# Seven-product tiles whose first product moves from one PSUM bank to another

## The chip, the cores and the metric

The kernel runs on one core of one Trainium2 chip. The metric is the time of one execution on the device in microseconds (us). TensorE (PE in the profile, with PEld for its weight loads) multiplies, VectorE (DVE) and ScalarE (ACT) do the elementwise work, GpSimd (POOL) and SyncE (SP) mostly issue DMAs.

## The reference

One inference step of a two-layer decoder on 512 prompt tokens and 8 sample tokens, width 1024, hidden width 2816. Each layer has two SwiGLU blocks around a token mixer, so there are four such blocks:

```python
def _swiglu(x, wg, wu, wd):
    return (jax.nn.silu(x @ wg) * (x @ wu)) @ wd
...
        x = x + 0.5 * _swiglu(_rmsnorm(x, norm_g[l, 0]), ffn_w_gate[l, 0], ffn_w_up[l, 0], ffn_w_down[l, 0])
        h = _rmsnorm(x, norm_g[l, 1])
        if l < N_A_LAYERS:
            out, nbuf = _pool_mixer(h, pool_bufs[l], pos0, pool_w[l], pool_scale[l])
...
            out = _window_attention(q, kk, vv, wb, pos0, attn_sinks[j]) @ w_o[j]
        x = x + out
        x = x + 0.5 * _swiglu(_rmsnorm(x, norm_g[l, 2]), ffn_w_gate[l, 1], ffn_w_up[l, 1], ffn_w_down[l, 1])
```

The change touches the four SwiGLU blocks alone; the pooling mixer, the attention and the norms stay as they are.

## The kernel before

Everything is held transposed: a tile has 128 features on the partitions and 520 tokens (512 + 8) in the free dimension; a half tile has 260 tokens (H). To keep float32 precision each operand is split into a high and a low part in the matmul's format, and a product of two blocks is three matmuls per 128 rows of the contraction: high by high, low by high, high by low. The weights are split as they arrive: ACT writes the high part (wh, line 287), DVE the low part (wl, line 288).

The hidden width of 2816 is 22 tiles, in three parts of 8, 8 and 6 (PARTS). The first 4, 3, 2 and 2 tiles of the four blocks are computed plainly (plain_tile). The others go through strassen_tile: it takes the gate and the up column block of a tile together as a 2 x 2 block matrix and multiplies it by the two token halves with seven block products instead of eight. The down projection of the parts of 8 tiles goes through strassen_down in the same manner, two output tiles at a time. One call of product is 12 matmuls of 128x260. In the order of the code the seven products are called, after their moving operand, B11, T1, T2, B21, B22, T3 and T4.

PSUM has eight banks, used as four pairs (duo). A tile takes two pairs: one bank of the first pair is a, in which B11, T2, T3 and T4 are accumulated one after the other; the second pair is c. B11 goes to a and ACT copies it to the first half of sa in SBUF (line 794, in strassen_down 831). T1 goes to the second bank of c and ACT copies it to sb (799, 833). T2 is accumulated onto a and ACT copies the sum to the second half of sa (802, 839). B21 goes to the first bank of c as a fresh sum, B22 is accumulated onto T1 in the second bank. Then DVE adds sa to both banks of c, 520 columns (806, 846), multiplies by the norm's factor R (809, 847), and ACT takes the silu (810); in strassen_down DVE adds the result to the residual instead (848). T3 is accumulated onto a, and DVE adds a to sb (812, 850). T4 is accumulated onto a after that, by a closure (rest) that runs when the next tile is under way; it ends in two DVE multiplications (815, 817; 855, 857), after which DVE and ACT make the operands of the down projection (hidden). The products onto a follow each other through its evacuations: T2 waits for the first copy, T3 for the second, T4 for the DVE addition to sb.

strassen_tile with early=True, the first such tile of each of the four blocks, goes another way, with one bank more.

Nothing in these blocks has an order written by hand. A scheduler takes the program, keeps its data dependences and its buffers, and lays the instructions of each engine out in an order of its own before the run; each engine then works through its list in order. So matmuls of several products are often woven into each other. Only the attention (PLAN) and some norms keep the written order.

Of the kernel before, what the change touches and what calls it, by code (L numbers as in the profile page):

```python
# [11 lines left out]
F32 = mybir.dt.float32  # L12
# [3 lines left out]
ALU = mybir.AluOpType  # L16
AX = mybir.AxisListType

P = 128
# [5 lines left out]
TOK = SP + NS  # L25
TW = TOK + NS
H = TOK // 2
# [297 lines left out]
def yoco_step(ctx, tc, ins, outs):  # L325
# [4 lines left out]
    V, S, T = nc.vector, nc.scalar, nc.tensor  # L330
# [19 lines left out]
    def duo():  # L350

        cnt[0] += 1
        return pools[0].tile([P, 2, 512], F32, tag="ps", name=f"ps{cnt[0]}")
# [178 lines left out]
    R = cp.tile([P, TOK], F32, name="R")  # L532

    def hcols(t, hf):
        return t[:, hf * H : (hf + 1) * H]


    def halves(t):
        return t.rearrange("p (h b a) -> p h b a", h=2, b=2)

    def two(z):

        return z.rearrange("p (b a) -> p a b", b=2)

    def back(z):

        return z.rearrange("p (b a) -> p b a", b=2)

    def outs(banks):

        return banks[:, :, :H].rearrange("p h (a b) -> p h b a", b=2)

    def out(bank):

        return bank[:, :H].rearrange("p (a b) -> p b a", b=2)
# [52 lines left out]
    def terms(w, xx):  # L608
        return ((w[0], xx[0]), (w[0], xx[1]), (w[1], xx[0]))
# [31 lines left out]
    def product(mov, bank, more=False):  # L641


        w = W.get()
        W.prefetch()
        for kk in range(4):
            for i, (a, b) in enumerate(terms(w, mov[kk])):
                T.matmul(  # L648
                    bank[:, :H],
                    a[:, kk, :],  # L650
                    two(b),
                    start=(not more and kk == 0 and i == 0),
                    stop=(kk == 3 and i == 2),
                    skip_group_check=more,
                )

    def hidden(g, hs):
        hs.take(g)
# [118 lines left out]
    def finish():  # L777
        if unfinished:
            unfinished.pop()()

    def strassen_tile(tmp, xx, tt, hs, early=False):

        B = lambda src, ks, hf: [tuple(hcols(z, hf) for z in src[k]) for k in ks]
        lo, up = range(4), range(4, 8)
        g = tmp.tile([P, TOK], F32, tag="g", name="g")
        t = tmp.tile([P, TOK], F32, tag="t", name="t")
        sa = tmp.tile([P, TOK], F32, tag="sa", name="sa")
        sb = tmp.tile([P, H], F32, tag="sb", name="sb", bufs=2)  # L790
        both, c = duo(), duo()
        a, b = both[:, 0, :], both[:, 1, :] if early else c[:, 1, :]
        product(B(xx, lo, 0), a)
        S.copy(back(hcols(sa, 0)), out(a))
        if early:
            product(B(xx, up, 0), c[:, 0, :])
            product(B(xx, up, 1), c[:, 1, :])
        product(B(tt, lo, 0), b)
        S.copy(back(sb), out(b))  # L799
        finish()  # L800
        product(B(tt, lo, 1), a, True)
        S.copy(back(hcols(sa, 1)), out(a))
        if not early:
            product(B(xx, up, 0), c[:, 0, :])
            product(B(xx, up, 1), c[:, 1, :], True)
        V.tensor_tensor(halves(g), halves(sa), outs(c), op=ALU.add)
        if early:
            V.tensor_tensor(hcols(g, 1), hcols(g, 1), sb, op=ALU.add)
        V.tensor_tensor(g, g, R, op=ALU.mult)
        S.activation(t, g, AF.Silu)  # L810
        product(B(tt, up, 0), a, True)
        V.tensor_tensor(back(sb), back(sb), out(a), op=ALU.add)

        def rest():
            V.tensor_tensor(hcols(g, 1), sb, hcols(t, 1), op=ALU.mult)
            product(B(tt, up, 1), a, True)
            V.tensor_tensor(back(hcols(g, 0)), out(a), back(hcols(t, 0)), op=ALU.mult)
            hidden(g, hs)

        unfinished.append(rest)  # L820

    def strassen_down(tmp, hs):

        b, st = hs.b, {}

        def head(i):
            a, c = duo()[:, 0, :], duo()
            sa = tmp.tile([P, TOK], F32, tag="sa", name="sa")
            sb = tmp.tile([P, H], F32, tag="sb", name="sb", bufs=2)
            product(b["B11"], a)  # L830
            S.copy(back(hcols(sa, 0)), out(a))
            product(b["T1"], c[:, 1, :])
            S.copy(back(sb), out(c[:, 1, :]))
            st[i] = a, c, sa, sb

        def second(i):
            a, c, sa, sb = st[i]
            product(b["T2"], a, True)
            S.copy(back(hcols(sa, 1)), out(a))

        def third(i):
            a, c, sa, sb = st[i]
            product(b["B21"], c[:, 0, :])
            product(b["B22"], c[:, 1, :], True)
            u = tmp.tile([P, TOK], F32, tag="u", name="u", bufs=nu[0])
            V.tensor_tensor(halves(u), halves(sa), outs(c), op=ALU.add)
            V.tensor_tensor(u, u, R, op=ALU.mult)
            V.scalar_tensor_tensor(x[2 * i], u, -0.5, x[2 * i], op0=ALU.mult, op1=ALU.add)
            product(b["T3"], a, True)
            V.tensor_tensor(back(sb), back(sb), out(a), op=ALU.add)  # L850

        def rest(i):
            a, c, sa, sb = st.pop(i)
            u = tmp.tile([P, TOK], F32, tag="u", name="u", bufs=nu[0])
            V.tensor_tensor(hcols(u, 1), sb, hcols(R, 1), op=ALU.mult)
            product(b["T4"], a, True)
            V.tensor_tensor(back(hcols(u, 0)), out(a), back(hcols(R, 0)), op=ALU.mult)
            V.scalar_tensor_tensor(x[2 * i + 1], u, 0.5, x[2 * i + 1], op0=ALU.mult, op1=ALU.add)

        head(0)  # L860
        finish()
        head(1)
        second(0)
        third(0)
        second(1)
        rest(0)
        third(1)
        for i in range(2, KT // 2):
            head(i)
            rest(i - 1)  # L870
            second(i)
            third(i)
        unfinished.append(lambda: rest(KT // 2 - 1))
# [24 lines left out]
    def ffn(fi, tmp, mov, hooks, tt, tags, after, before_last=None, first=None, by_parts=None, hold=False):  # L898

        j = 0  # L900
        for pi, n in enumerate(PARTS):
# [3 lines left out]
            for _ in range(n):  # L905
                if j == 0 and first is not None:
                    plain_end(tmp, *first, hs)
                elif j < NPL[fi]:
                    plain_tile(tmp, mov, hs, hooks)
                else:  # L910
                    while hooks:
                        hooks.pop(0)()
                    strassen_tile(tmp, mov, tt, hs, j == NPL[fi])
                j += 1
                W.pin = lambda ins: ins
# [1198 lines left out]
```

## Time and profile before

| | |
|---|---|
| Median of 3 runs | 1533.73 us (1533.15 to 1533.79) |
| The profiled execution's own time | 1532.24 us |
| Its span, first to last instruction | 1530.5 us |
| PE busy | 1507.7 us (99%), 13338 matmuls |
| DVE busy | 1406.7 us (92%), 2791 instructions |
| ACT busy | 969.2 us (63%), 2030 instructions |
| POOL busy | 309.6 us (20%) |
| TensorE clock granted | 0.999 of full speed |
| DMA | 255.43 MB, mean 167 GB/s |

An engine's busy time is the time in which at least one of its instructions runs. A matmul of 128x260 is shown with a duration of about 0.28 us, but the next starts about 0.11 us after it, so PE also counts as busy in short gaps between starts: the starts say more than the busy share. Likewise a DVE instruction on 520 columns is shown with about 0.70 us, and the next may start 0.60 us after it. A row "A <- B" of the waits says that A's engine was idle and that B ended the idleness.

### The profile page before, as it was taken

To read this page: it belongs to the slowest core of one execution; us is meant where nothing else is said; L and a number is where in the kernel's file an instruction comes from. 1 tells how busy PE (TensorE), PEld (TensorE's weight loads), DVE (VectorE), ACT (ScalarE), POOL (GpSimd) and SP (SyncE) were. 2 spreads that over 40 slices of the span, in tenths; PEclk is the share of its full clock that TensorE was granted. 3 is DMA by queue.
4 is the path that set the end of the run, shared out by engine and by line. 5 is a ranking of instruction groups with operands and counts; after the bars stand their busy time and mean duration, and the time that the engine had idled before them with its cause. 6 is when DMAs were issued, how large, how long until landed. Compare 5 with 4: busy or idle time off the path is not lost. (4 is left out here: it accounts for less than half of the span.)

```text
span 1530.5 us, 35121 instructions
## 1 busy us (share of the span) xinstructions
PE 1507.7 (99%) x13338; PEld 1492.0 (97%) x13338; DVE 1406.7 (92%) x2791; ACT 969.2 (63%) x2030; POOL 309.6 (20%) x348
## 2 busy tenths in 40 slices
PE   9999999999999999999999999999999999999997
PEld 9999999999999999999999999999999999999997
DVE  6999999979999999989899999987897999999976
ACT  6765665657665665656665665655886765665555
POOL 1122222101121222100321222201561122222200
PEclk9999999999999999999999999999999999999999
DMA  9689989754688989845889998953334588998941
GB/s 248 123 190 200 190 190 200 182 170 119 139 196 182 196 193 196 176 129 129 206 188 193 189 199 188 183 173 88 86 72 103 126 178 188 196 192 191 197 133 57
DMA packets 420037, 255.43 MB, mean 167 GB/s; under 512 B 13182, under 2 KB 400246, under 8 KB 419828
## 3 DMA queue, kind: packets, MB, share of 16 engines
q1 hardware_dynamic: 339918, 187.56, 44.5%
q0 software_dynamic: 76192, 60.53, 28.2%
q10 hardware_dynamic: 3758, 5.09, 1.1%
q8 instruction: 105, 1.72, 0.5%
q14 instruction: 64, 0.52, 0.1%
HBM read 218.59 MB, written 6.11 MB: 147 GB/s over the span
## 5 line engine op out<-in xcount | busy, mean ns | idle before, releaser
L287 ACT ACTIVATE wh<-raw 128x512 fp32r<-128x512 f32 (+1 forms) x770 | 445.7, 616 | 242.2 <-DVE raw L221 80.0
L288 DVE TENSOR_TENSOR wl<-raw,wh 128x512 fp32r<-128x512 f32 (+1 forms) x770 | 503.0, 679 | 37.9 <-ACT wh L287 34.3
L648 PE MATMUL ps<-th,wh 128*128 128x260 f32 x1232 | 338.5, 276 | 0.6 <-ACT sb L799 0.4
L648 PE MATMUL ps<-th,wl 128*128 128x260 f32 x1232 | 337.2, 275 | 0.5 <-DVE wl L288 0.5
L648 PE MATMUL ps<-tl,wh 128*128 128x260 f32 x1232 | 337.6, 275 | 0.0
L648 PE MATMUL ps<-xh,wh 128*128 128x260 f32 x908 | 248.8, 276 | 1.2 <-ACT wh L287 0.9
L648 PE MATMUL ps<-xh,wl 128*128 128x260 f32 x908 | 248.3, 275 | 0.5 <-DVE wl L288 0.4
L648 PE MATMUL ps<-xl,wh 128*128 128x260 f32 x908 | 248.2, 275 | 0.0
L648 PEld LDWEIGHTS ps<-th,wh 128*128 128x128 f32 x1232 | 234.0, 190 | 2.0 <-ACT wh L287 0.9
L648 PEld LDWEIGHTS ps<-tl,wh 128*128 128x128 f32 x1232 | 234.1, 190 | 0.0
L648 PEld LDWEIGHTS ps<-th,wl 128*128 128x128 f32 x1232 | 233.3, 190 | 0.7 <-DVE wl L288 0.7
L398 POOL DMA_DIRECT2D S<-in_ffn_w_up_dram x77 | 102.2, 1327 | 429.3 <-DMA S<-in_ffn_w_up_dram 130.8
L648 PE MATMUL ps<-hh,wh 128*128 128x260 f32 x656 | 180.1, 278 | 3.5 <-ACT wh L287 1.7
L648 PE MATMUL ps<-hl,wh 128*128 128x260 f32 x656 | 179.2, 276 | 0.9 <-DVE hl L380 0.9
L648 PE MATMUL ps<-hh,wl 128*128 128x260 f32 x656 | 178.3, 275 | 0.0
L214 POOL DMA_DIRECT2D raw<-raw x109 | 96.1, 882 | 399.1 <-DVE wl L288 122.2
L648 PEld LDWEIGHTS ps<-xh,wh 128*128 128x128 f32 x908 | 172.2, 190 | 2.2 <-ACT wh L287 1.5
L648 PEld LDWEIGHTS ps<-xh,wl 128*128 128x128 f32 x908 | 171.9, 190 | 1.0 <-DVE wl L288 1.0
L648 PEld LDWEIGHTS ps<-xl,wh 128*128 128x128 f32 x908 | 172.2, 190 | 0.1
L648 PEld LDWEIGHTS ps<-hh,wh 128*128 128x128 f32 x656 | 124.0, 190 | 5.5 <-ACT wh L287 2.3
L648 PEld LDWEIGHTS ps<-hl,wh 128*128 128x128 f32 x656 | 124.2, 190 | 1.6 <-DVE hl L380 1.6
L648 PEld LDWEIGHTS ps<-hh,wl 128*128 128x128 f32 x656 | 123.9, 190 | 0.0
(369 smaller groups left out, 3608.1 us busy)
## 6 DMA issues: line engine op xcount, KB each, us to landing
raw<-in_ffn_w_gate_dram SPq DMA_DIRECT2D x87, 512.0 KB, 4.5
raw<-in_ffn_w_up_dram SPq DMA_DIRECT2D x87, 512.0 KB, 6.4
raw<-in_ffn_w_down_dram SPq DMA_DIRECT2D x128, 256.0 KB, 5.0
raw<-raw POOLq DMA_DIRECT2D x109, 256.0 KB, 4.2
S<-in_ffn_w_up_dram SPq DMA_DIRECT2D x77, 256.0 KB, 4.7
S<-in_ffn_w_up_dram POOLq DMA_DIRECT2D x77, 256.0 KB, 5.6
raw<-in_ffn_w_down_dram SPq DMA_DIRECT2D x16, 768.0 KB, 4.3
S<-in_ffn_w_down_dram SPq DMA_DIRECT2D x32, 256.0 KB, 3.1
```

The lines of the kernel that those rows point to most:

```text
L214: G.dma_start(blk(raw, 2, 1), blk(raw, 1, 1), accum_op=ALU.add)
L287: pin(nc.scalar.activation(dh, src, AF.Copy))
L288: pin(nc.vector.tensor_tensor(dl, src, dh.bitcast(F32), op=ALU.subtract))
L398: return [ld(lambda t: t, a), lambda t: nc.gpsimd.dma_start(t, b, accum_op=ALU.add)]
L648: T.matmul(bank[:, :H], a[:, kk, :], two(b), start=(not more and kk == 0 and i == 0), stop=(kk == 3 and i == 2), skip_group_check=more,)
```

## The change

In the seven-product tiles other than the early ones, the first copy of ACT no longer goes to SBUF but to the first bank of c, and B21 is accumulated onto it instead of starting a fresh sum. The second copy, of B11 + T2, goes to SBUF as before. DVE then adds it to the second bank of c only, in place, 260 columns instead of 520, and the multiplication by R reads both banks of c from PSUM (520 columns) instead of a tile in SBUF. The copies keep the order of the columns as it lies in the bank instead of changing it; the multiplication changes it. Of 77 calls of strassen_tile four are early and stay as they are, so 73 tiles change there and 32 in strassen_down, 105 in all.

```diff
         product(B(xx, lo, 0), a)
-        S.copy(back(hcols(sa, 0)), out(a))
         if early:
+            S.copy(back(hcols(sa, 0)), out(a))
             product(B(xx, up, 0), c[:, 0, :])
             product(B(xx, up, 1), c[:, 1, :])
+        else:
+            S.copy(c[:, 0, :H], a[:, :H])
         product(B(tt, lo, 0), b)
         S.copy(back(sb), out(b))
         finish()
         product(B(tt, lo, 1), a, True)
...
+        else:
+            S.copy(hcols(sa, 1), a[:, :H])
+            product(B(xx, up, 0), c[:, 0, :], True)
             product(B(xx, up, 1), c[:, 1, :], True)
+            V.tensor_tensor(c[:, 1, :H], hcols(sa, 1), c[:, 1, :H], op=ALU.add)
+            V.tensor_tensor(halves(g), outs(c), halves(R), op=ALU.mult)
...
             product(b["B11"], a)
-            S.copy(back(hcols(sa, 0)), out(a))
+            S.copy(c[:, 0, :H], a[:, :H])
             product(b["T1"], c[:, 1, :])
...
-            product(b["B21"], c[:, 0, :])
+            product(b["B21"], c[:, 0, :], True)
             product(b["B22"], c[:, 1, :], True)
             u = tmp.tile([P, TOK], F32, tag="u", name="u", bufs=nu[0])
-            V.tensor_tensor(halves(u), halves(sa), outs(c), op=ALU.add)
-            V.tensor_tensor(u, u, R, op=ALU.mult)
+            V.tensor_tensor(c[:, 1, :H], sa, c[:, 1, :H], op=ALU.add)
+            V.tensor_tensor(halves(u), outs(c), halves(R), op=ALU.mult)
```

The number of instructions is the same on every engine. The order on SP is the same, POOL's differs in a few rows; PE's, DVE's and ACT's were laid out anew by the scheduler, since c is now written first by ACT and the DVE additions are shorter.

What changes in the waits: c is one tile of two banks for the program's tracking of dependences, and its first writer is now the copy. In all 105 tiles the first matmul of T1, which writes the other bank of c, waits for the count that the copy's end raises. Before, no matmul into c waited for a copy. Here is PE's list at the end of B11 and the start of T1, in a tile of the second block whose a is ps_7822 and whose c is ps_7823. Before:

```order
L648 MATMUL ps_7822<-xh,wh 128x260
L648 MATMUL ps_7822<-xl,wh 128x260
L648 MATMUL ps_7822<-xh,wl 128x260
L648 MATMUL ps_7823<-th,wh 128x260 [waits DVE_49]
L648 MATMUL ps_7823<-tl,wh 128x260
L648 MATMUL ps_7823<-th,wl 128x260
```

T1 follows B11 without a wait for ACT. In the changed kernel:

```order
L648 MATMUL ps_7822<-xh,wh 128x260
L648 MATMUL ps_7822<-xl,wh 128x260
L648 MATMUL ps_7822<-xh,wl 128x260
L648 MATMUL ps_7823<-th,wh 128x260 [waits DVE_49,Activation_49]
L648 MATMUL ps_7823<-tl,wh 128x260
L648 MATMUL ps_7823<-th,wl 128x260
```

The rows are the same, and the first of T1 now waits for ACT's copy of what the row above it completes. Of the 105 tiles, 19 have no matmul of another product between the end of B11 and the start of T1, one has 1, one has 3, 12 have 7, one has 10, and the others 12 or more. (Before, 44 tiles had none there either, and in 44 others T1 was begun ahead of B11's end.)

The second place is PE's list at the end of B22 in the last output tiles of a strassen_down in the second block (a is ps_8974, c is ps_8975; ps_9115 and ps_9116 are a and c of the next tile). Before:

```order
L648 MATMUL ps_8975<-hh,wl 128x260
L648 MATMUL ps_9115<-xh,wh 128x260 [waits PE_49,Activation_49]
L648 MATMUL ps_9115<-xl,wh 128x260
L648 MATMUL ps_9116<-th,wh 128x260 [waits PE_49,Activation_49]
L648 MATMUL ps_9116<-tl,wh 128x260
L648 MATMUL ps_9115<-xh,wl 128x260 [waits DVE_49]
```

In the changed kernel:

```order
L648 MATMUL ps_8975<-hh,wl 128x260
L648 MATMUL ps_9115<-xh,wl 128x260 [waits DVE_49]
L648 MATMUL ps_9115<-xh,wh 128x260
L648 MATMUL ps_8974<-ph,wh 128x260 [waits Activation_49]
L648 MATMUL ps_8974<-pl,wh 128x260
L648 MATMUL ps_8974<-ph,wl 128x260
```

Before, B11, T1 and T2 of the next tile were woven in here, so that 48 matmuls stood between the end of B22 and the start of T4. In the changed kernel T3 follows at once, then eight matmuls of the next tile, and T4 stands 22 matmuls after the end of B22. That is so in 12 tiles of strassen_down and in 25 of strassen_tile. Before, four tiles had 22 or fewer and the other 101 had 32 or more.

T4 waits for DVE's addition of a to sb, and this is DVE's list at the same place, before:

```order
L846 TENSOR_TENSOR u<-sa,ps_8975 128x520 [waits PE_49,Activation_49]
L847 TENSOR_TENSOR u<-u,R 128x520 [waits DVE_49]
L288 TENSOR_TENSOR wl<-raw_8801,wh 128x512 [waits Activation_49]
L850 TENSOR_TENSOR sb<-sb,ps_8974 128x260 [waits PE_49]
L848 SCALAR_TENSOR_TENSOR x_87<-u,x_87 128x520 [waits DVE_49]
```

and in the changed kernel:

```order
L851 TENSOR_TENSOR ps_8975<-sa,ps_8975 128x260 [waits PE_49]
L852 TENSOR_TENSOR u<-ps_8975,R 128x520 [waits DVE_49]
L288 TENSOR_TENSOR wl<-raw_8801,wh 128x512 [waits Activation_49]
L853 SCALAR_TENSOR_TENSOR x_87<-u,x_87 128x520 [waits DVE_49]
L855 TENSOR_TENSOR sb<-sb,ps_8974 128x260 [waits PE_49]
```

The addition to sb, on which T4 waits, moved behind the addition to the residual. In the 25 tiles of strassen_tile the list from the addition to c (813) to the addition to sb (817) is L813, L814, a split L288 and L817, with the split in the second or the third place.

More of the change, by code (lines that the diff above doesn't have):

```diff
@@ L801, in strassen_tile @@
         product(B(tt, lo, 1), a, True)
-        S.copy(back(hcols(sa, 1)), out(a))
-        if not early:
-            product(B(xx, up, 0), c[:, 0, :])
+        if early:
+            S.copy(back(hcols(sa, 1)), out(a))
+            V.tensor_tensor(halves(g), halves(sa), outs(c), op=ALU.add)
+            V.tensor_tensor(hcols(g, 1), hcols(g, 1), sb, op=ALU.add)
+            V.tensor_tensor(g, g, R, op=ALU.mult)
+        else:
+            S.copy(hcols(sa, 1), a[:, :H])
+            product(B(xx, up, 0), c[:, 0, :], True)
             product(B(xx, up, 1), c[:, 1, :], True)
[L806 to L809, printed above, removed]
+            V.tensor_tensor(c[:, 1, :H], hcols(sa, 1), c[:, 1, :H], op=ALU.add)
+            V.tensor_tensor(halves(g), outs(c), halves(R), op=ALU.mult)
         S.activation(t, g, AF.Silu)
@@ L827, in head @@
             a, c = duo()[:, 0, :], duo()
-            sa = tmp.tile([P, TOK], F32, tag="sa", name="sa")
+            sa = tmp.tile([P, TOK], F32, tag="sa", name="sa")[:, :H]
             sb = tmp.tile([P, H], F32, tag="sb", name="sb", bufs=2)
             product(b["B11"], a)
-            S.copy(back(hcols(sa, 0)), out(a))
+            S.copy(c[:, 0, :H], a[:, :H])
             product(b["T1"], c[:, 1, :])
@@ L838, in second @@
             product(b["T2"], a, True)
-            S.copy(back(hcols(sa, 1)), out(a))
+            S.copy(sa, a[:, :H])
         def third(i):
             a, c, sa, sb = st[i]
-            product(b["B21"], c[:, 0, :])
+            product(b["B21"], c[:, 0, :], True)
             product(b["B22"], c[:, 1, :], True)
             u = tmp.tile([P, TOK], F32, tag="u", name="u", bufs=nu[0])
-            V.tensor_tensor(halves(u), halves(sa), outs(c), op=ALU.add)
-            V.tensor_tensor(u, u, R, op=ALU.mult)
+            V.tensor_tensor(c[:, 1, :H], sa, c[:, 1, :H], op=ALU.add)
+            V.tensor_tensor(halves(u), outs(c), halves(R), op=ALU.mult)
             V.scalar_tensor_tensor(x[2 * i], u, -0.5, x[2 * i], op0=ALU.mult, op1=ALU.add)
```

## The prediction

> **What bounds the kernel now.** I read the page's first part, then the waits of PE, then the busy times by stretch, then the groups of the instructions that change, then two short pieces of the timeline.
>
> ```profile
> span 1530.5 us, 35121 instructions
> PE 1507.7 (99%) x13338; PEld 1492.0 (97%) x13338; DVE 1406.7 (92%) x2791; ACT 969.2 (63%) x2030; POOL 309.6 (20%) x348
> ```
>
> PE is full, so only what makes PE wait can change the time, and nothing that is taken off DVE or ACT pays by itself. These are PE's longest waits at the seven-product line 648, and ACT's for PE at the first copy:
>
> ```profile
> PE ps L648 <- ACT wh L287: 2.6, 3, 0.9
> PE ps L648 <- DVE wl L288: 1.0, 2, 0.5
> PE ps L648 <- DVE hl L380: 0.9, 2, 0.5
> PE ps L648 <- DVE g L817: 0.8, 3, 0.3
> PE ps L648 <- ACT sa L839: 0.7, 3, 0.2
> ...
> ACT sa L794 <- PE ps L648: 57.7, 42, 2.1
> ```
>
> They are few and short. Where they lie shows in the busy times by stretch (PE, PEld, DVE, ACT and POOL, us and number of instructions, then the clock, the DMA share and GB/s). Two quiet stretches first, then the eight stretches where one part of a block goes over into its down projection:
>
> ```profile
> 465.00:559.00 94.00, 94.00 (x844) 94.00 (x843) 91.77 (x171) 56.95 (x115) 20.56 (x19) 1.00 0.89 191
> 110.00:200.00 90.00, 90.00 (x809) 90.00 (x808) 87.81 (x163) 55.41 (x113) 20.57 (x19) 1.00 0.93 199
> ...
> 64.00:107.00 43.00, 41.29 (x359) 40.29 (x358) 42.92 (x84) 28.94 (x61) 10.06 (x10) 1.00 0.92 188
> 203.00:239.00 36.00, 35.96 (x313) 35.16 (x312) 35.83 (x69) 21.83 (x47) 8.16 (x8) 1.00 0.89 196
> 404.00:464.00 60.00, 58.24 (x509) 57.19 (x508) 58.72 (x115) 41.04 (x85) 12.21 (x11) 1.00 0.77 163
> 559.00:595.00 36.00, 35.96 (x312) 35.16 (x312) 35.83 (x68) 21.75 (x47) 8.74 (x8) 1.00 0.91 198
> 800.00:825.00 25.00, 24.97 (x219) 24.59 (x219) 24.93 (x49) 14.77 (x32) 6.55 (x6) 1.00 0.90 192
> 888.00:940.00 52.00, 50.57 (x439) 49.34 (x439) 50.86 (x97) 32.98 (x69) 12.51 (x12) 1.00 0.93 195
> 1264.00:1298.00 34.00, 32.60 (x281) 31.56 (x280) 33.06 (x63) 20.58 (x43) 8.48 (x8) 1.00 0.91 192
> 1379.00:1414.00 35.00, 33.60 (x289) 32.57 (x289) 33.99 (x65) 20.64 (x43) 8.73 (x8) 1.00 0.91 195
> sum 321.00, PE 313.19 PEld 305.84 DVE 316.15 ACT 202.53 POOL 75.44; mean PE 39.15 PEld 38.23 DVE 39.52 ACT 25.32 POOL 9.43
> ```
>
> In the quiet stretches a matmul starts every 94/844 = 0.111 us: PE loses nothing there. In the eight others 321 us would hold 2881 matmuls at that pitch, and they hold 2721: PE loses 160 x 0.111 = 17.8 us. DVE is busy for 316.15 of these 321 us, so there it sets the pace. This 17.8 us is the most that a relief of DVE can give back.
>
> **The change, part by part.** First what DVE saves (duration in ns ahead of the second bar; the columns after x are the count, the sum in us and the mean):
>
> ```profile
> L806 DVE TENSOR_TENSOR g<-sa,ps 128x520 f32<-128x520 f32 x77 | 53.5, 695 | 1.1 <-PE ps L648 0.8
> L809 DVE TENSOR_TENSOR g<-g,R 128x520 f32<-128x520 f32 x77 | 53.9, 700 | 0.0
> L812 DVE TENSOR_TENSOR sb<-sb,ps 128x260 f32<-128x260 f32 x77 | 32.6, 424 | 0.0
> L815 DVE TENSOR_TENSOR g<-sb,t 128x260 f32<-128x260 f32 x77 | 33.0, 430 | 4.5 <-ACT t L810 1.5
> L926 DVE TENSOR_TENSOR u<-ps,R 128x520 f32<-128x520 f32 x29 | 20.2, 698 | 6.4 <-PE ps L620 6.4
> ```
>
> The multiplication out of PSUM is of the very form of L926, 698 ns against L809's 700: nothing lost. The addition goes from 695 ns to 260 columns, for which L812 (one operand in PSUM) stands, 424 ns. No DVE instruction of before writes to PSUM, so its price is bounded by 424 below and by the 695 of the old form above; I take 424, since L812 and L815 show that PSUM or SBUF as a source makes no difference. A tile saves 0.27 us, 105 tiles 28.5 us of DVE's 1406.7.
>
> [...]
>
> What the relief is worth: 30 additions of the forms L806 and L846 lie in the eight stretches, two of them early, so 28 x 0.27 = 7.6 us are taken off DVE where it sets the pace. In the quiet stretches DVE's saving buys nothing directly, as PE starts a matmul every 0.111 us there already; at most DVE enters a stretch with less left over. I give that 1.5 us, between 0 and the 7.6 of the stretches themselves.
>
> Second, the new wait: T1 behind the copy of B11. This is what a wait of PE for such a copy looks like (start and duration in us), PE and then ACT:
>
> ```profile
> 101.31 0.28 PE L648 MATMUL ps<-xh,wl 128*128 128x260 f32 x1
> 101.42 0.28 PE L648 MATMUL ps<-xl,wh 128*128 128x260 f32 x1
> 101.54 0.28 PE L648 MATMUL ps<-xh,wl 128*128 128x260 f32 x1
> 102.09 0.38 PE L648 MATMUL ps<-hh,wh 128*128 128x260 f32 x1 [0.28 <-ACT sa L831]
> 102.31 0.28 PE L648 MATMUL ps<-hl,wh 128*128 128x260 f32 x1
> ...
> 101.14 0.63 ACT L287 ACTIVATE wh<-raw 128x512 fp32r<-128x512 f32 x1 [0.37 <-PE ps L648]
> 101.68 0.36 ACT L831 COPY sa<-ps 128x260 f32<-128x260 f32 x1
> ```
>
> The copy ends at 102.04 and PE starts at 102.09, so a hop between engines takes 0.05 us. The matmul after the wait takes 0.22 us to the next start instead of 0.11. With nothing in between, PE's last matmul ends 0.28 us after its start, the copy starts 0.05 later, takes 0.37, and T1 starts 0.05 after it: 0.75 us instead of 0.11, and 0.11 more behind it, 0.75 us lost. No row shows a copy from PSUM to PSUM; 0.37 of L794 is the row of the same size, and if ACT is late by a split (0.54 us from 101.14 to 101.68) the price is 1.29. ACT was waiting for PE at 42 of the 77 copies, so I take 0.75.
>
> The order has 19 places with no matmul in between, one with 1 (0.64) and one with 3 (0.42); at 7 matmuls (0.78 us) the copy is just hidden. By their places in the list 9 of the 19 lie in the eight stretches and 10, with the other two, in quiet ones. Quiet: 10 x 0.75 + 0.64 + 0.42 = 8.6 us, in full on the path, up to 15 if ACT is late each time.
>
> Third, T4 moves to 22 matmuls behind B22 in 37 tiles, and waits for DVE's addition to sb. Two pitches of DVE, one independent and one dependent:
>
> ```profile
> 233.79 0.70 DVE L848 SCALAR_TENSOR_TENSOR x<-u,x 128x520 f32<-128x520 f32 x1
> 234.40 0.70 DVE L858 SCALAR_TENSOR_TENSOR x<-u,x 128x520 f32<-128x520 f32 x1
> ...
> 109.84 0.69 DVE L846 TENSOR_TENSOR u<-sa,ps 128x520 f32<-128x520 f32 x1
> 110.56 0.70 DVE L847 TENSOR_TENSOR u<-u,R 128x520 f32<-128x520 f32 x1
> ```
>
> Independent 520 columns follow at 0.61, a dependent one 0.03 after the end. In strassen_down (12 tiles): 0.28 + 0.05 from B22's last start to DVE, 0.45 for the addition to c, then 0.61, 0.60 and 0.61 for the multiplication, the split and the residual, and 0.42 + 0.05 for the addition to sb: 3.07 us. T4 would be due after 23 x 0.111 = 2.56, so it is 0.51 late, with the slower restart 0.62. Eight of the 12 lie in the stretches, four (2.5 us) in quiet ones. In strassen_tile (25 tiles) the residual isn't there: 2.46 us, or 2.35 where the split stands second, against 2.56. That just fits, and any lateness of DVE goes to PE. I take 0.1 us each, 2.5 us, between 0 and the 15 that one more DVE instruction of 0.60 in front would make.
>
> In the stretches the new waits are 9 x 0.75 + 8 x 0.62 = 11.7 us. They do not add up with what is lost there now: while PE waits for a copy, DVE catches up. The ends are -7.6 (the waits fall into the old ones and the relief passes through) and +11.7 (neither). I take 0, below the middle, because DVE's 316 of 321 us say that it sets most of the pace.
>
> The rest costs nothing: ACT has as many copies of the same size and is busy 63%; one copy in each strassen_down also waits for DVE to free c, but that DVE instruction stands three products (4 us) ahead; SP's order is the same, and earlier freed buffers meet DMA engines at 0.77 to 0.93, so transfers hardly gain.
>
> Sum: 8.6 + 2.5 + 2.5 + 0 - 1.5 = **+12.1 us**. On the profiled execution (1532.24 us, span 1530.5 and 1.7 around it) that is 1544.3; the median of the runs is 1.5 above it, so I predict 1545.8 us.
>
> **The rivals.** *Faster.* The eight stretches lose nothing any more (-17.8): PE's new waits there give DVE all the time that it lacks. With the 11.1 us of the quiet places, that gives 1527. For it speaks DVE's share there; against it that the wait for ACT's L287 is the longest in PE's list, and that DVE gains but 7.6 us. It decides in favour of faster from the point where the stretches give back over 14.2 us (11.1 and 3.1).
>
> *No change.* The relief passes through in the stretches (-7.6) and DVE's head start is worth 3 us: 8.6 + 2.5 - 7.6 - 3 = 0.5, 1534 us. Against it: T1's wait in quiet stretches has no cover, whatever DVE does.
>
> *Much slower.* ACT does its copy a split late at the 19 bare places and the 12 that have 7 matmuls: 31 x 0.54 = 17 us more, 1563 us; with half of them late, 1554. ACT was late at 35 of 77 copies before, but then by less than a whole split. The same comes of a DVE write to PSUM at 0.695 us, with 0.27 more in all 37 tight tiles, 10 us: 1556. [...]
>
> **How the numbers follow.** 0.2% of the time is 3.1 us, about what can be told from no change. Forecast (4 to 19 us slower) 0.66; much slower 0.15; no change 0.12; faster 0.07. So slower 0.81, same 0.12, faster 0.07. The range goes from 1533, which takes in most of the no-change case and the low end in the stretches, to 1560, with half of the much-slower case; some 2 in 10 are left out.
>
> **What the profile after would show.** Waits of PE for ACT's copies (lines 799 and 836), some twenty, each with about 0.45 us idle shown, and the copy starting as B11 ends: step two. Waits for the addition to sb at 855, a dozen of about 0.35 idle, and few at 817: step three. DVE's busy time down by about 28 us, the addition to c at about 424 ns: step one. The two quiet stretches no longer at 0.111 us for each matmul; the loss in the eight stretches about as before. I am wrong if PE shows hardly any wait for those copies, if the stretches lose much less than 17.8 us, or if the addition in PSUM takes far more than 424 ns.

## The result: 19 us slower, and the profile after

The changed kernel takes 1552.61 us (median of 4 runs, 1551.33 to 1554.24), the kernel before beside it 1533.44 (1531.46 to 1533.79): a ratio of 1.0126, 95% interval 1.0113 to 1.0139. The forecast was 1545.8, range 1533 to 1560, so the sign and the range held and the size was 7 us short. The profiled execution took 1554.24 us, against 1532.24 before. Its page begins:

```profile
span 1552.4 us, 35098 instructions
PE 1514.1 (98%) x13338; PEld 1495.3 (96%) x13338; DVE 1390.7 (90%) x2791; ACT 984.9 (63%) x2030; POOL 309.6 (20%) x348
```

DVE is busy 16 us less, and PE 6 us longer though it does the same matmuls. PE's waits, longest first (us in total, times, longest):

```profile
PE ps L648 <- ACT ps L836: 6.8, 16, 1.0
PE ps L648 <- ACT ps L799: 6.0, 12, 1.3
PE ps L648 <- DVE sb L855: 4.4, 13, 0.3
PE pv L576 <- DVE acc L991: 1.6, 1, 1.6
```

The first three rows are new. Lines 799 and 836 are the copies of B11 into bank 0 of c, and in all 28 places the matmul that waits is T1's first; line 855 is the addition to sb, and in all 13 the waiting matmul is T4's first. The groups that changed:

```profile
L814 DVE TENSOR_TENSOR g<-ps,R 128x520 f32<-128x520 f32 x73 | 50.8, 697 | 0.7
L813 DVE TENSOR_TENSOR ps<-sa,ps 128x260 f32<-128x260 f32 x73 | 31.5, 432 | 4.4 <-PE ps L648 2.3
L799 ACT COPY ps<-ps 128x260 f32<-128x260 f32 x73 | 26.5, 363 | 41.4 <-PE ps L648 41.2
L836 ACT COPY ps<-ps 128x260 f32<-128x260 f32 x32 | 11.7, 365 | 28.1 <-PE ps L648 26.2 <-DVE x L853 1.9
```

No operation is dear: the addition in PSUM takes 432 ns, the multiplication out of PSUM 697, the copy between banks 363 and 365. One wait for the copy, on PE and then on ACT:

```profile
501.96 0.28 PE L648 MATMUL ps<-xh,wl 128*128 128x260 f32 x1
502.68 0.38 PE L648 MATMUL ps<-th,wh 128*128 128x260 f32 x1 [0.45 <-ACT ps L799]
502.90 0.28 PE L648 MATMUL ps<-tl,wh 128*128 128x260 f32 x1
...
502.27 0.36 ACT L799 COPY ps<-ps 128x260 f32<-128x260 f32 x1 [1.88 <-PE ps L648]
```

ACT sat idle until B11's last matmul ended and copied at once; PE starts T1 0.72 us after the start before instead of 0.11, and its second matmul 0.22 after that: 0.72 us late for 0.45 us of shown idle. To add this up I take all starts of the product line in the timeline and sum how much later each comes than 0.1113 us for every matmul since the start before. I call it the lateness of the product line. It is 22.5 us before and 38.9 after, so 16.4 of the 21.9 us between the two spans arise in the seven products. The rows that show a wait for the bank copies hold 17.4 us of it, those for line 855 6.5, and neither was there before. For its place I take the same matmuls, counted from the start, in both traces. The eight transition stretches then hold 20 us of lateness before and 18 after; with their edges moved by a few us it is 20 and up to 23. So most or all of the 16.4 us lies in the quiet stretches, that is, everywhere else. These are two of them (columns as in the prediction):

```profile
467.00:559.00 92.00, 90.65 (x807) 90.08 (x806) 87.17 (x165) 56.70 (x114) 19.68 (x18) 1.00 0.88 186
112.00:200.00 88.00, 86.93 (x769) 86.09 (x769) 84.38 (x161) 53.79 (x108) 19.71 (x18) 1.00 0.91 193
```

At the pitch of before (94/844 us) these 180 us would hold 1616 matmuls; they hold 1576.

The other 5.5 us lie outside that line. The largest piece, 1.9 us net, is near 350 us, where PE waited 1.56 us for acc (line 991), and behind that wait the clock was lowered (0.83 is the granted clock):

```profile
350.00:360.00 10.00, 8.44 (x59) 8.24 (x58) 8.00 (x24) 5.97 (x17) 0.64 (x1) 0.83 0.22 29
360.00:370.00 10.00, 10.00 (x88) 10.00 (x86) 9.40 (x21) 8.08 (x20) 0.00 (x0) 1.00 0.52 151
```

Before, the clock was 1.00 there. Part of the 5.5 us belongs to the execution and not to the kernel: the profiled one is the slowest of the four (1554.24 us against a median of 1552.61), the one of before was faster than its median (1532.24 against 1533.44), and first_in_c below, whose PE list is the same row for row, has only 2.0 us more outside the line than the kernel before.

### The profile page after: what moved, and what is told of

Same layout as the page of the kernel before. It is cut to its first block, busy times and chain, and to the rows that moved or that the text cites. A ratio compares the mean times of both kernels' runs of the same rounds, so it can differ in the third digit from the quotient of the medians.

```text
span 1552.4 us, 35098 instructions
## 1 busy us (share of the span) xinstructions
PE 1514.1 (98%) x13338; PEld 1495.3 (96%) x13338; DVE 1390.7 (90%) x2791; ACT 984.9 (63%) x2030; POOL 309.6 (20%) x348
## 5 line engine op out<-in xcount | busy, mean ns | idle before, releaser
L287 ACT ACTIVATE wh<-raw 128x512 fp32r<-128x512 f32 (+1 forms) x770 | 458.0, 618 | 317.5 <-PE ps L648 140.6
L288 DVE TENSOR_TENSOR wl<-raw,wh 128x512 fp32r<-128x512 f32 (+1 forms) x770 | 508.3, 677 | 62.2 <-ACT wh L287 49.6
```

What stands on the lines that cost most here:

```text
L287: pin(nc.scalar.activation(dh, src, AF.Copy))
L288: pin(nc.vector.tensor_tensor(dl, src, dh.bitcast(F32), op=ALU.subtract))
```

## Experiments

All against the kernel before, with profiled spans and lateness (in the product line, as above) side by side. Each ratio is to runs of the kernel before that were made beside that kernel's (medians 1532.62 to 1533.44 us):

| kernel | median us | ratio to before, 95% | span | lateness |
|---|---|---|---|---|
| before | 1533.44 | 1 | 1530.5 | 22.5 |
| changed | 1552.61 | 1.0126 (1.0113 to 1.0139) | 1552.4 | 38.9 |
| relief_alone | 1528.04 | 0.9971 (0.9961 to 0.9981) | 1526.3 | 14.5 |
| wait_alone | 1580.33 | 1.0312 (1.0298 to 1.0325) | 1578.2 | 64.3 |
| copy_behind_t1 | 1539.80 | 1.0050 (1.0037 to 1.0063) | 1538.0 | 29.5 |
| copy_behind_sb | 1564.53 | 1.0204 (1.0189 to 1.0220) | 1562.9 | 52.1 |
| first_in_c | 1553.31 | 1.0125 (1.0109 to 1.0140) | 1547.2 | 37.2 |
| residual_later | 1552.19 | 1.0126 (1.0113 to 1.0139) | 1548.4 | 37.9 |
| sb_first | 1548.36 | 1.0101 (1.0086 to 1.0116) | 1548.1 | 34.7 |
| first_in_c_sb_first | 1548.99 | 1.0103 (1.0087 to 1.0120) | 1547.2 | 33.6 |
| copy_twice | 1569.01 | 1.0233 (1.0219 to 1.0246) | 1566.3 | 52.9 |
| t1_first | 1540.52 | 1.0048 (1.0036 to 1.0061) | 1537.0 | 23.0 |
| t1_first_sb_first | 1536.36 | 1.0020 (1.0011 to 1.0029) | 1535.6 | 21.9 |
| second_as_before | 1535.42 | 1.0017 (1.0008 to 1.0026) | 1531.7 | 21.7 |

Span less lateness is 1508 to 1514 us in all of them: the lateness of this one line explains the differences but for some 6 us. Most edits also make the scheduler lay PE's list out anew, so such a run tests its edit together with a new order.

My theory was the prediction's: PE loses time where T1 stands bare behind the copy, and where T4 stands too near behind B22. The rivals: operations on PSUM are dear in themselves, or the lateness would come anyway under another name.

**The relief without the wait.** B11 goes to SBUF again; the rest of DVE's saving stays.

```diff
-            S.copy(c[:, 0, :H], a[:, :H])
+            S.copy(back(hcols(sa, 0)), out(a))
...
-            product(B(xx, up, 0), c[:, 0, :], True)
+            product(B(xx, up, 0), c[:, 0, :])
```

> The changed kernel without the copy from bank to bank and without accumulation onto it: B11 is copied to the SBUF tile sa as in the kernel before, and B21 starts bank 0 of c afresh. VectorE adds 260 columns in PSUM and multiplies straight out of PSUM as in the changed kernel. It leaves out the addition of B11 to the first half of the output. My theory: without the wait for the copy what is left is VectorE's relief, worth between 0 and 7.6 us: 1526 to 1535 us. Rival A (operations on PSUM cost PE its banks for longer): 1545 to 1552. Rival B (the relief of 28 us counts in full): about 1505 to 1515.

Measured 1528.04 us, 0.3% faster than before. Its longest waits in the product line:

```profile
PE ps L648 <- ACT wh L287: 1.1, 3, 0.5
...
PE ps L648 <- DVE g L814: 0.7, 1, 0.7
```

No wait for the first copy is left, and one for sb. DVE's additions in PSUM and multiplications out of PSUM are all there, so rival A falls. The lateness is 8.0 us below before's, not 28, so rival B falls too. As the order of PE is another as well, no run separates what the relief alone gives.

**The wait without the relief.** The kernel before with the bank copy, B21 accumulated, and DVE's old addition of 520 columns and multiplication in SBUF.

```diff
+            S.copy(c[:, 0, :H], a[:, :H])
...
+            product(B(xx, up, 0), c[:, 0, :], True)
...
+            V.tensor_tensor(halves(g), twice(hcols(sa, 1)), outs(c), op=ALU.add)
```

> The other half: B11 is copied from bank to bank and B21 and B22 accumulate in c, so T1 waits for the copy, but VectorE's work is that of the kernel before (one addition of 520 columns out of PSUM into SBUF, then one multiplication in SBUF). For this the second copy is added to both halves, so the second half gets what it should and the first half gets one product too many. In the emitted order T1 stands directly behind B11 (0 or 1 matmuls between) in 57 tiles, against 20 in the changed kernel, and T4 22 matmuls or nearer behind B22 in 36, against 37. My theory (each bare place costs 0.72 us, save where PE is late anyway): 57 x 0.72 = 41 us if all count, 25 if four in ten lie where PE waits for weights; with T4's 5 us that is 1560 to 1580 us, some 57 waits of 0.45 us idle for the bank copy. Rival (the copy's wait is cheap and the additions in PSUM are what cost): 1533 to 1538 us.

Measured 1580.33 us, at the upper end of the theory.

```profile
PE ps L652 <- DVE sb L822: 14.9, 28, 1.3
PE ps L652 <- ACT ps L801: 12.4, 27, 0.9
PE ps L652 <- ACT ps L841: 3.1, 6, 0.7
```

33 waits for the bank copy, not 57, with 20.9 us of lateness; and 28 of T4 for sb (line 822 here), 19.4 us, where I had allowed 5. So the total came out right by two errors: of the 57 near places only 33 waited, and T4, 22 matmuls behind B22, was 0.7 us late each time with DVE's longer addition in front. In the changed kernel T4 waits at one place of strassen_tile (line 817). That fits a relief that pays there, by keeping this T4 in time; as the two orders differ, it is not shown. Six waits for the copy to sb (2.8 us of idle) and five of strassen_down's T4 (2.1) came besides.

**T1 as the first writer of c.** The same line, moved behind T1's product, and then behind the copy to sb as well (the first is shown, in strassen_down; in strassen_tile it is alike):

```diff
-            S.copy(c[:, 0, :H], a[:, :H])
             product(b["T1"], c[:, 1, :])
+            S.copy(c[:, 0, :H], a[:, :H])
             S.copy(back(sb), out(c[:, 1, :]))
```

> The changed kernel with one line moved in each of the two seven-product functions: the copy of B11 into bank 0 of c is written behind T1's product, so that T1 is the first to write the duo c and doesn't wait for the copy; only B21 does, and in the emitted order at least 12 matmuls lie between T1 and B21. All VectorE savings stay, and B22's last matmul stands at least 24 ahead of T4's first, against 22 in 37 tiles. My theory (the loss is T1's wait for the copy, 0.72 us at some 20 places, and T4 standing too near behind B22): both go, 1528 to 1538 us, and PE's idle before its product line with a copy as releaser falls from 12.8 us to under 2. Rival A (the loss is the price of the additions and multiplications that now read and write PSUM on VectorE, in the order they were already in): they all stay, about 1550 us. Rival B (of the two parts only T1's wait counts for little, the rest is the order that the planner chose): 1540 to 1550.

> As copy_behind_t1, but the copy to bank 0 of c is written behind the copy to sb too. T1 waits for no copy; in PE's list T1 stands directly behind B11 in 52 tiles without a wait, T4 at least 24 behind B22. In copy_behind_t1 PE waited 23 times for a high part of a weight (12.5 us of lateness, 3.1 before), which no edit there asked for. My theory (those come with the order that the scheduler found for that program, not with the copy): another order has them in another number, and the time falls between relief_alone and copy_behind_t1, 1528 to 1540 us, by 0.6 us for each such wait. Rival (a copy that waits for T1 holds up the splits behind it on ACT, whatever the order): 20 or more such waits again, 1539 to 1542 us.

Measured 1539.80 and 1564.53 us. Of the first, and then of the second:

```profile
PE ps L648 <- ACT wh L287: 8.7, 23, 1.2
PE ps L648 <- ACT ps L800: 1.9, 2, 1.4
```

```profile
PE ps L648 <- ACT wh L287: 8.3, 19, 1.2
PE ps L648 <- ACT ps L801: 7.9, 16, 1.8
PE ps L648 <- DVE wl L288: 6.6, 12, 0.7
```

In copy_behind_t1 T1 waits for no copy and T4 never for sb, and 12.8 us are gone. But I missed the range: 23 waits for high parts of weights (12.5 us) have come in their place, all at the first matmul of a B11. In its lists 86 weights are used 17 or fewer matmuls after PE frees the buffer that they are written to, against none below 18 in the changed kernel. In copy_behind_sb 16 first matmuls of T2 wait for the copy, which now stands behind the copy to sb on ACT, and the weights are late 31 times. Neither expectation held there: it was slower than both. The order that the scheduler lays out decides more than the line that was moved.

**The copy the other way round.** B11 is multiplied into bank 0 of c and copied to a (shown for strassen_down; strassen_tile is alike).

```diff
-            product(b["B11"], a)
-            S.copy(c[:, 0, :H], a[:, :H])
+            product(b["B11"], c[:, 0, :])
+            S.copy(a[:, :H], c[:, 0, :H])
```

> The changed kernel with B11 and the copy turned round: B11 is multiplied into bank 0 of c, where B21 is later accumulated onto it, and ACT copies it from there to a, where T2 is accumulated. The first writer of c is PE again, so T1 waits for no copy; T2 does, as it did in the kernel before, with 9 or more matmuls between. The lists of PE, VectorE, GpSimd and SyncE are those of the changed kernel instruction for instruction (but for the bank's name), and ACT's differ in the operands of the 105 copies alone. So T4 still stands 22 matmuls behind B22 in 37 tiles. My theory: exactly T1's waits go, which are 17.4 us of lateness in the trace of the changed kernel (28 rows of 0.6 us): 1534 to 1538 us, and the 13 waits for the addition to sb stay as they are. Rival A (something else is late at the same places and takes the wait over): 1540 to 1550. Rival B (the copy from bank to bank is dear in itself): 1549 to 1553.

Measured 1553.31 us: no change, and my expectation was wrong in its premise.

```profile
PE ps L648 <- ACT ps L836: 6.7, 16, 1.0
PE ps L648 <- ACT ps L799: 6.0, 12, 1.3
PE ps L648 <- DVE sb L855: 4.2, 12, 0.3
```

The same 28 waits stand at the same place, T1's first matmul. T1 no longer follows a write of c, but it follows a read, and c is tracked as one tile: a write to its second bank waits for the copy that reads the first. PE's list is the changed kernel's, row for row, and so is the loss. So a read of c's other bank that stands between B11 and T1 holds T1 up as the write did.

**T4 and the residual.** The residual update of x[2i] behind the addition to sb, first by the order of the code alone, then with the order of the two fixed by later() (the second is shown; the first has the same lines without it):

```diff
-            V.scalar_tensor_tensor(x[2 * i], u, -0.5, x[2 * i], op0=ALU.mult, op1=ALU.add)
             product(b["T3"], a, True)
-            V.tensor_tensor(back(sb), back(sb), out(a), op=ALU.add)
+            later(V.tensor_tensor(back(sb), back(sb), out(a), op=ALU.add))
+            later(V.scalar_tensor_tensor(x[2 * i], u, -0.5, x[2 * i], op0=ALU.mult, op1=ALU.add))
```

> The changed kernel with one line moved in strassen_down alone: the residual update of x[2i] is written behind T3 and the addition to sb that T4 waits for, so that VectorE does the addition to sb first. PE's order and T1's waits stay as they are (18 bare places against 19). My theory: the 12 places where PE idles 0.35 us (0.62 us late) for the addition to sb go: 7 us less at most, 1545 to 1549 us, and PE's idle for that line falls from 4.4 us to under 1. Rival (the tile is late through something else that comes next, such as the g or x line, or the weights): the idle moves to another line and the time stays at 1551 to 1554.

> The changed kernel with the order of two VectorE instructions of strassen_down fixed: the addition to sb, then the residual update of x[2i]. In residual_later the lines were turned round in the code, but VectorE's list still had the residual update ahead in 29 of 32 tiles; here it has the addition ahead in all 32. PE's list changes with it: T1 directly behind B11 in 11 tiles against 19, T4 22 matmuls behind B22 in 40 against 37. My theory (the residual update of 0.69 us between is what makes the addition late): the 13 waits of 0.35 us idle (6.5 us) go, and with 8 bare places fewer another 5: 1540 to 1546 us. Rival (the addition is late through the splits wl and the two operations on c ahead of it): idle for that line stays over 3 us, 1546 to 1552.

residual_later took 1552.19 us, no change: the scheduler put the residual update ahead again, so the edit tested nothing. sb_first took 1548.36. PE's waits there, then DVE's list at one of the 15:

```profile
PE ps L648 <- DVE sb L854: 4.2, 15, 0.3
PE ps L648 <- ACT ps L836: 3.2, 8, 1.0
```

```profile
244.46 0.43 DVE L851 TENSOR_TENSOR ps<-sa,ps 128x260 f32<-128x260 f32 x1 [0.70 <-PE ps L648]
244.80 0.68 DVE L288 TENSOR_TENSOR wl<-raw,wh 128x512 fp32r<-128x512 f32 x1
245.41 0.69 DVE L852 TENSOR_TENSOR u<-ps,R 128x520 f32<-128x520 f32 x1
246.01 0.68 DVE L288 TENSOR_TENSOR wl<-raw,wh 128x512 fp32r<-128x512 f32 x1
246.61 0.42 DVE L854 TENSOR_TENSOR sb<-sb,ps 128x260 f32<-128x260 f32 x1
```

The residual is out of the way, and a second split of a weight has taken its place ahead of the addition. The rival held: here too four DVE instructions stand ahead of the addition, and T4 is late. The 4.2 us that were gained go with the eight waits that left line 836 (9.4 to 4.5 us of lateness), since fewer T1 stand bare.

> Both edits: B11 in bank 0 of c and copied to a, and the addition to sb ahead of the residual update. My theory: T1's waits and most of T4's are gone, and what is left beside the kernel before is VectorE's relief: 1526 to 1532 us, faster than before. Rival (T4 still stands 22 behind B22 in 40 tiles and waits for the multiplication or the splits instead): 1532 to 1537.

1548.99 us, as sb_first, with the same PE list: first_in_c adds nothing to it, as it did nothing alone.

**More cover by a longer copy.** The copy of B11 twice, one behind the other:

```diff
             S.copy(c[:, 0, :H], a[:, :H])
+            S.copy(c[:, 0, :H], a[:, :H])
```

> The changed kernel with the copy of B11 into bank 0 of c made twice, one behind the other, with the same values. ACT has 105 copies of 0.36 us more, and T1 must wait for the second. But the scheduler, which then sees a longer copy, puts other matmuls between: T1 stands directly behind B11 in 2 tiles against 19, and 10 or more behind it in all the others (the nearest group 12 matmuls, 1.34 us, against 0.83 + 0.36 = 1.19 us from B11's last start for the two copies). T4 stays 22 behind B22 in 39 tiles, against 37. My theory (the loss is the matmuls that are missing between B11 and T1, not the copy): 28 waits for the copy fall to under 6, 13 to 16 us go, 1536 to 1542 us, although more work is done. Rival (the copy between banks is dear in itself, for ACT or for PE's banks): it costs twice as much, 1556 to 1575 us.

1569.01 us: the theory's number failed, and the rival's fits, but not for its reason.

```profile
PE ps L648 <- DVE sb L857: 8.4, 16, 0.7
PE ps L648 <- ACT ps L799: 6.3, 14, 0.5
PE ps L648 <- ACT ps L800: 4.5, 3, 2.8
```

T1's waits are 3 instead of 28 (the third row). The first two rows are T4's: in the program the 14 matmuls of the second row are T4's first, which wait for the addition to sb and a weight. That the row names the copy is an inference of the profile, since in most of them the copy ends about 0.05 us ahead of the start. The addition to sb (line 818) ends 0.15 us ahead in all 14, just as the one of line 857 does in the first row's waits of 0.7 us, where the last copy ended 0.31 us ahead. The 12 matmuls that cover the copy are T4 of the tile before, pulled nearer to the addition that it waits for. Cover given to T1 was taken from T4. Eight new waits for the copy to sb (3.2 us of idle) came besides.

**T1 ahead of B11.** T1's product is written first, with the two weights swapped in the plan of weights, so that B11 is on PE while nothing touches c:

```diff
+            product(b["T1"], c[:, 1, :])
             product(b["B11"], a)
-            S.copy(c[:, 0, :H], a[:, :H])
-            product(b["T1"], c[:, 1, :])
             S.copy(back(sb), out(c[:, 1, :]))
+            S.copy(c[:, 0, :H], a[:, :H])
```

> The changed kernel with T1's product written ahead of B11's in all seven-product tiles but the early ones (the two weights swapped in the plan of weights too); the copy to sb comes first, then the copy of B11 into bank 0 of c. T1 is c's first writer and waits for no copy. T2 waits for the copy, 12 or more matmuls behind B11 in 93 tiles, 2 to 5 in 10. T4 stands 32 or more behind B22 in all tiles. My theory (both waits gone, VectorE's relief left): 1526 to 1534 us. Rival (the weights are late, as in copy_behind_t1, where 86 weights had 17 or fewer matmuls between the release of their buffer and their use and PE waited 20 times more than before, 12.5 us; here 70 have): 1536 to 1542 us.

> t1_first with the addition to sb fixed ahead of the residual update on VectorE in strassen_down. T2 then stands 12 or more matmuls behind B11 in 102 tiles, and 40 weights have 17 or fewer matmuls between release and use. My theory: 1525 to 1532 us, a little under t1_first. Rival (late weights): half the number of t1_first's, 1532 to 1537 us.

> t1_first_sb_first, but in the tile right behind an early one B11 is written ahead of T1 again (four tiles), with the copy of B11 still behind the copy to sb. In the trace of t1_first_sb_first PE waits three times 0.99 to 1.06 us for ACT's copy to sb in the early tile, 3.5 us of lateness, where the kernel before waited 0.43, since the next tile's T1 has taken the place of its B11 as cover. My theory: these fall to about 0.6 us of lateness each, 1.8 us less, 1533 to 1536 us, level with the kernel before. Rival (what is left above the kernel before lies outside the tiles, in the norm that waits for acc and the clock that is lowered behind it): 1535 to 1538 us, no change against t1_first_sb_first.

1540.52, 1536.36 and 1535.42 us. Of the first, and then of the third:

```profile
PE ps L648 <- ACT wh L287: 4.4, 9, 0.9
PE ps L648 <- ACT sb L801: 3.0, 3, 1.1
PE pv L576 <- DVE acc L993: 2.8, 1, 2.8
```

```profile
PE ps L648 <- ACT wh L287: 2.2, 3, 1.5
PE ps L648 <- ACT sb L803: 2.2, 3, 0.9
PE pv L576 <- DVE acc L995: 1.3, 1, 1.3
```

With the copy, the accumulation and all of DVE's saving in place, no wait for the bank copy is left, and the lateness is that of the kernel before (23.0, 21.9, 21.7 against 22.5). So the lateness that the change brought goes with the waits of T1 and T4. Whether the copy and the accumulation cost anything else is not shown: relief_alone, without them and in another order, has 7 us of lateness less, and some 3 of these are the early tile's waits for sb.

The first two times lie in the rivals' ranges, above mine. The late weights came in t1_first (nine waits, 5.9 us, against three of 3.1 before) and largely went with sb_first, as expected. But they are not why the times are above mine, since the lateness didn't rise: span less lateness is 1514.0 and 1513.7 us against 1508.0 before, so what these two profiled executions lose against the kernel before lies outside the product line. The rivals' numbers fit more by luck than for their reason. In the third the waits for the early tile's sb shrank from 3.0 to 2.2 us of idle; its 0.9 us against the second can't be told from none, and both of its ranges hold it. None of the three is faster than the kernel before: they give up 7 us of lateness against relief_alone, and I found no order that keeps the copy and reaches its time.

## Why the prediction was right, and where it was not

- *What bounds.* Right, as far as shown: relief_alone, with DVE's saving of 28 us and another order, has 8.0 us less lateness; the prediction had put the saving's worth in the eight stretches at 7.6 at most. The loss in these stretches before is 20 us and not 17.8: the counts of the rows include two or three matmuls a stretch that only reach over its edge.
- *DVE's prices.* Right: 432 ns for the addition (424 taken), 697 for the multiplication (698 taken); 105 x (0.695 - 0.432) = 27.6 us of durations, against 28.5. The multiplication took 700 ns out of SBUF before, so the PSUM source made it no dearer here. The *busy time* fell by 16 us instead of 28. It counts a stretch once where two instructions overlap: the durations of all DVE instructions sum to 33 us less (1615.5 to 1582.1), and 17 us less of them overlap (208.8 to 191.4).
- *T1's wait.* The mechanism and its price were right: 0.45 us of shown idle forecast, 0.45 measured at most places, 0.72 us of lateness against 0.75. Mis-sized was the count: 28 waits, against 21, with 18 of them in the eight stretches, against 9. Six of the extra ones stand where 7 matmuls lie between B11 and T1, at the start of each strassen_down, where the copy was to be just hidden. There ACT is still at two splits of the hidden values when B11 ends, and T1 waits 0.27 to 0.34 us:

```profile
817.23 0.93 ACT L379 ACTIVATE xh<-g 128x260 fp32r<-128x260 f32 x2
818.07 0.37 ACT L836 COPY ps<-ps 128x260 f32<-128x260 f32 x1
...
818.49 0.38 PE L648 MATMUL ps<-xh,wh 128*128 128x260 f32 x1 [0.27 <-ACT ps L836]
```

- *ACT late.* Two other waits are the case of the rival *much slower* (1.00 and 1.26 us of idle). With the six above that is 8 of the 31 places that it needed, so it fell.
- *T4.* Right in number and price: 13 waits of up to 0.35 us for line 855 (a dozen of 0.35 forecast), one at line 817. The place was wrong: by the count of matmuls all 13 lie outside the eight stretches, six of them within 4 us behind an end, where the kernel before lost next to nothing that they could stand in for. The prediction had eight of the 12 inside and so left them out of the sum.
- *The stretches.* Net 0 forecast, between -2 and +3 measured, by where the edges are put. The new waits in them hold 11 us (13 with the slower restarts), and yet the stretches lose about what they lost before: the two don't add up, as the prediction argued. That they cancel almost exactly was a guess between -7.6 and +11.7, which held.
- *The sum.* +12.1 forecast, +19.2 measured between the medians and 21.9 between the profiled spans. The new waits in the quiet stretches hold 16 us: ten of T1 7.2, against 8.6 forecast, and 14 of T4 9.0, against 5.0, restarts included. So T4 is the term of the tiles that was too small, by its place. The head start of DVE (1.5 us) shows nowhere: lateness there beside these waits is some 5 us, against 2.5 before. The 5.5 us of the profiled pair outside the product line, where I had 0, are in part the spread between executions; how much of them the change brings stays open.
- *Faster* and *no change* fell by the same rows. They needed the stretches to give back more than the quiet places take. Both took 11.1 us for the quiet places where the sum has 13.6 (they leave out the 2.5 of strassen_tile), so each should stand 2.5 us higher.

## What to carry to other kernels

A copy that is the same size and no dearer than the one that it replaces (363 ns against 369) can still cost, if it puts another engine's instruction on a tile between two products: look at which instruction then waits, and whether anything stands between. In this program dependences are tracked by the tile, and a write or a read of one bank held up the product into the other bank (28 waits of T1 in the changed kernel, 28 in first_in_c). Writing the independent product first (T1 ahead of B11) took these waits away where turning the copy round did not, though the kernel came out no faster than before the change. The relief of DVE bought far less than its size (27.6 us of durations; relief_alone, with another order too, is 4.6 us faster than before), and cover for one wait was taken from another (copy_twice: 3 waits of T1 instead of 28, and 30 of T4 instead of 14): follow the matmuls that fill it.

## What was not expected of the hardware and the order

The lowered clock near 350 us, in the changed kernel, on PE:

```profile
351.32 0.28 PE L1216 MATMUL pv<-th,xl 128*128 128x256 f32 x1
353.16 1.28 PE L576 MATMUL pv<-ones,acc 128*128 128x1 f32 x10 [1.56 <-DVE acc L991]
354.30 0.37 PE L1216 MATMUL pv<-th,xh 128*128 128x256 f32 x1
...
355.12 0.42 PE L1216 MATMUL pv<-th,xl 128*128 128x256 f32 x1
355.34 0.41 PE L1216 MATMUL pv<-th,xh 128*128 128x256 f32 x1
...
358.27 0.28 PE L1216 MATMUL pv<-th,xl 128*128 128x256 f32 x1
358.38 0.28 PE L1216 MATMUL pv<-th,xh 128*128 128x256 f32 x1
```

Between 351.3 and 354.3 us PE has only ten matmuls of one column. From 354.9 to 358.2 the next start then comes after 0.21 us instead of 0.12: about half the rate for some 3.4 us, which costs 1.5 us. The granted clock of the stretch from 354.9 to 358.3 us is 0.52, and the 0.83 of the ten us fits a clock of one half for 3.4 of them. The same pause doesn't always bring it, which I had not expected either. In relief_alone PE waited 1.51 us at this place and the clock stayed at 1.00; in second_as_before it was 0.84 over the ten us from 350, behind a wait of 1.30, and in t1_first 0.66, behind a wait of 2.8. What decides it, no run here shows. The pause itself also comes and goes: first_in_c has the same PE list, but in its profiled execution PE didn't wait for acc and the clock stayed at 1.00; it ran in 1549.02, 1553.23, 1553.40 and 1553.44 us, the profiled one being the first.

A copy between banks took about as long as one from a bank to SBUF: 363 and 365 ns, against 359 (line 810) in the same trace, all of 260 columns.
